# One PSUM bank request of the latents' attention, moved from the attention's banks to the projections' banks

## The chip, the cores and the metric

The kernel runs on one core of a Trainium2 chip. The metric is device time in microseconds (us) of one execution, from the first to the last instruction of the core with the little that lies around it. The time that is compared is the median of several executions.

## The reference

One inference step of a hybrid backbone with two layers. 128 context (prompt) tokens and 256 latent tokens share all weights. Each layer is a mixing sublayer (attention, a bidirectional mLSTM and a pooling, side by side, then one output projection) and a PEER expert sublayer:

```python
for l in range(DEPTH):                       # 2 layers
    h = rmsnorm(x) * (1 + scale1) + shift1
    x += gate1 * W_out[attention(h) | mlstm(h) | pool(h)]
    h = rmsnorm(x) * (1 + scale2) + shift2
    x += gate2 * peer(h)                     # 8 heads, top 16 of 16384 experts
y = rmsnorm(x)
```

What the change touches is the attention of the latents. 8 query heads share 2 key heads of width 64, the latents are two tiles of 128 tokens, and each tile attends to its own tile, to its neighbour under a band mask and to 128 cached context keys:

```python
s_band = einsum('bnqkgd,bnskd->bnkgqs', qb, kb) * scale    # masked outside the window
s_ctx  = einsum('bnqkgd,bpkd->bnkgqp', qb, kc) * scale
p = softmax_with_sink(concatenate([s_band, s_ctx], -1), sink)
o = p[..., :nband] @ vb + p[..., nband:] @ vc
```

The prompt tokens read only prompt tokens.

## The kernel before

**Stages.** For each layer `mixing` (line 352) computes the mixing sublayer for both groups of tokens, and also the prompt's half of the PEER routing; then come the latents' queries, scores and routing, and a dense PEER pass over all 16384 experts for the latents. In the dense pass TensorE multiplies blocks of 128 experts with all latents, while the prompt's 128 tokens are served by gathers on the GpSimd queue (`experts`, line 839) that are cut into small pieces and put between the other work.

**The order of the work.** `mixing` is a dictionary of steps, and two strings, `ORDER0` and `ORDER1` (lines 40 and 41), name the order in which the steps are written for layer 0 and layer 1. The steps that matter here: `att1` and `att2` are the attention of the two latent tiles, `att0` that of the prompt; `mem0`, `mem1`, `mem2` the mLSTM of the three tiles; `pool0`, `pool1` the pooling of the prompt and of the latents; `mix0` and `mix1` the output projection of the prompt and of the latents; `norm` the second norm of the prompt; `ask` the prompt's PEER queries and their top 16 (four groups, each a projection, a transposition and a score product); `route` the prompt's expert choice; `&mod1`, `mod1` and the like the modulation vectors, which stream 16 blocks of `w_mod` each; `+20` and the like run so many pieces of the prompt's experts. The strings are

```python
ORDER0 = "np ns kv c q gate qk ox | &mod1 mod1 mem2 mem0 mem1 att0 pool0 &mod2 att1 att2 pool1 mod2 &next0 mix0 spill norm ask mix1 next0 route +20 +3 +6 +3 +3"
ORDER1 = "np ns q c gate kv att0 qk ox &mod1 mod1 | mem0 pool0 &mod2 mod2 mix0 norm ask mem1 att1 spill route +5 +15 att2 mem2 pool1 +15 +10 mix1 +4"
```

The written order is a priority, not the final order: a planner (the tile framework's list scheduler with a timeline of its own) puts the instructions of each engine in a fixed order, earlier written ones first among those that are ready, and adds the waits. On the chip each engine runs its list in that order.

**PSUM.** A bank is 128 x 512 fp32. In the mixing stage the eight banks are four tags (`BANKS`, line 36): `at` with three, `pm` with one (modulation), `p` with three, `m` with one. `bank(tag, name)` (line 91) asks for a bank of a tag, and the planner hands it out when the tile is first written and takes it back after the last read. `p` serves the projections (`project` with its default tag), and by the step table `mem0`, `pool0`, `mix0`, `norm` and `ask`; `m` serves `mem1`, `mem2` and `pool1`; `at` serves `ns`, the query and key transposes, `att0`, `att1`, `att2` and `mix1`.

**The attention** is `attention(i, tag)` (line 640). For a latent tile it makes four passes, one for each of 2 key heads and 2 pairs of query heads. A pass is called a step below. A step takes two banks for the scores S (one per head, lines 664 to 668, each 128 x 384 with the mask added by a matmul), finds the row maxima on VectorE (668), forms the shift (670 to 672), exponentiates on ScalarE with the sum on the side (676), scales by the reciprocal sum on VectorE (681), transposes the six 128 x 128 blocks of probabilities on TensorE into two more banks PT (685 to 689), copies them to SBUF on ScalarE (690), and multiplies them with the values into the output bank `po`, written oT in the profile (692). `po` is held for all four steps of a tile. P has two SBUF buffers for the latents and PT three (`LAYOUT`).

**Other rings.** Weights pass through four raw buffers (`raw`), then are split by ScalarE (`hi`, line 105) and VectorE (`lo`, line 106) into four buffers each. The blocks of `w_mod` use the same four raw buffers. `rsqrt` (line 183) takes small tiles of tags `rs_v`, `rs_t` (two each) and `rs_r` (three).

Of the kernel before, what the change touches and what calls it, by code (L numbers as in the profile page):

```python
# [68 lines left out]
def tile_hybrid_step(ctx: ExitStack, tc: tile.TileContext, I, O):  # L69
# [21 lines left out]
    def bank(tag, name):  # L91
        tag = ALSO.get(tag, tag)
        pool, n = OPEN[tag]
        return pool.tile([P, 512], F32, tag=tag, bufs=n, name=name)
# [84 lines left out]
    def tsl(i):  # L179
        return slice(i * P, (i + 1) * P)  # L180
# [171 lines left out]
    def mixing(l, p1, rooms, silu):  # L352
# [169 lines left out]
        def mix_out(s, k0, k1, c, src):  # L522
            if s and mixT[1] is None:
                early.append((s, k0, k1, c, src))
                return
            if mixT[0] is None:
                mixT[0] = prompt_T(f"mixp{l}")
            split_into(*[t[:, k0:k1, c] for t in mixT[s]], src)
# [111 lines left out]
        def attention(i, tag):  # L640
            n = f"{i}{l}"
            room = rooms[min(i, 1)]
            ka = kaT[0] if i == 0 else kaT[1]
            vs = [kv[0][:, P:2 * P]] if i == 0 else [kv[1][:, P:2 * P], kv[2][:, P:2 * P], cv]
            nkp = len(vs)
            nk = nkp * P
            po = bank(tag, f"oT{n}")
            nh = 2 if i else 4
            for g in range(2):
                gs = slice(g * 64, g * 64 + 64)  # L650
                for j0 in range(0, 4, nh):
                    m = f"{n}{g}{j0}"
                    small = lambda tag: p1.tile([P, 4], F32, tag=f"{tag}{min(i, 1)}", bufs=2, name=f"{tag}{m}")[:, :nh]
                    mx, nm, es, sums = small("amx"), small("anm"), small("aes"), small("asum")
                    heads = []
                    if i == 0:
                        b = bank(tag, f"S{m}")
                        for j in range(4):
                            pe.matmul(b[:, tsl(j)], qaT[gs, j, tsl(i)], ka[gs, :], start=True, stop=True)
                            heads.append(b[:, tsl(j)])  # L660
                        ve.reduce_max(mx, b.rearrange("p (j k) -> p j k", j=4), axis=AX.X)
                    else:
                        for j in range(nh):
                            b = bank(tag, f"S{m}{j}")
                            pe.matmul(b[:, :nk], qaT[gs, j0 + j, tsl(i)], ka[gs, :], start=True, stop=False)
                            pe.matmul(b[:, tsl(2 - i)], identb, mskb[:, i - 1, :], start=False, stop=True)
                            heads.append(b[:, :nk])
                            ve.reduce_max(mx[:, j:j + 1], b[:, :nk], axis=AX.X)
                    sk = sinkb[:, g * 4 + j0:g * 4 + j0 + nh]
                    ve.scalar_tensor_tensor(nm, mx, 0.125, sk, op0=ALU.mult, op1=ALU.max)  # L670
                    ve.tensor_scalar_mul(nm, nm, -1.0)
                    ve.tensor_add(es, sk, nm)
                    ac.activation(es, es, AF.Exp)
                    Pt = room.tile([P, nh, nk], F32, "P", f"P{m}")
                    for j in range(nh):
                        ac.activation(Pt[:, j, :], heads[j], AF.Exp, bias=nm[:, j:j + 1], scale=0.125,
                                      accum_out=sums[:, j:j + 1])
                    ve.tensor_add(sums, sums, es)
                    ve.reciprocal(sums, sums)
                    for j in range(nh):  # L680
                        ve.tensor_scalar_mul(Pt[:, j, :], Pt[:, j, :], sums[:, j:j + 1])
                    PT = room.tile([P, nkp, nh * P], F32, "PT", f"PT{m}")
                    per = 512 // (nh * P)
                    for k0 in range(0, nkp, per):
                        b = bank(tag, f"PT{m}{k0}")
                        kps = range(k0, min(nkp, k0 + per))
                        for kp in kps:
                            for j in range(nh):
                                pe.transpose(b[:, tsl((kp - k0) * nh + j)], Pt[:, j, tsl(kp)], ident)
                        ac.copy(PT[:, k0:k0 + len(kps), :], b[:, 0:len(kps) * nh * P].rearrange("p (k x) -> p k x", k=len(kps)))  # L690
                    for kp in range(nkp):
                        pe.matmul(po[gs, j0 * P:(j0 + nh) * P], vs[kp][:, gs], PT[:, kp, :], start=(kp == 0),
                                  stop=(kp == nkp - 1), skip_group_check=True)
            mix_out(min(i, 1), 0, 4, tsl(max(i - 1, 0)), po.rearrange("p (j t) -> p j t", j=4))
# [35 lines left out]
        def mix(tiles, tag):  # L730
            room = rooms[min(tiles[0], 1)]
            g = gate_row(room, l, 0, min(tiles[0], 1))
            for h in range(2):
# [14 lines left out]
               for g, c in enumerate(cols) for w, t in who.items()},  # L748
            "|": collect,
            **{f"att{i}": (lambda i=i: attention(i, "at" if i else ATT0)) for i in range(3)},  # L750
            **{f"mem{i}": (lambda i=i: mlstm(i, "m" if i else "p")) for i in range(3)},
            "pool0": lambda: pooling(0, "p"),
# [591 lines left out]
```

## Time and profile before

| | us |
|---|---|
| median of 3 executions | 2735.05 |
| lowest, highest | 2731.38, 2752.36 |
| profiled execution, its own time | 2746.87 |
| its span, first to last instruction | 2745.1 |
| TensorE (PE) busy | 2500.7 (91%) |
| VectorE (DVE) busy | 1722.4 (63%) |
| ScalarE (ACT) busy | 1045.5 (38%) |
| GpSimd (POOL) busy | 927.6 (34%) |
| mean granted TensorE clock | 0.944 |

The profiled execution lies 11.8 us above the median and inside the span of the three times. Layer 0's mixing stage takes roughly the first 347 us, layer 1's roughly 1400 to 1717 us; the changed line runs at 176 to 282 us and 1500 to 1621 us. A busy TensorE is not one at its peak: matmuls overlap and their ends are modelled. "Granted clock" is the share of full TensorE speed.

### The profile page before, as it was taken

Reading aid. Unit: us, or ns where it says so; the run is one execution under the profiler, and the core shown is the slowest. Engines: PE = TensorE matmul, PEld = TensorE weight load, DVE = VectorE, ACT = ScalarE, POOL = GpSimd, SP = SyncE. Lnnn points to the kernel's source line nnn. Section 1 sums busy time; section 2 is a strip of 40 time slices with the busy share of each in tenths; the row PEclk is TensorE's granted clock in tenths of the full one; section 3 lists DMA queues with packets and bytes.
Section 4 is the critical chain, followed back from the end, with each engine's and each line's share of the span. In section 5 each row is a group of like instructions: output and inputs, shape, how many; then the busy total and the mean of one; then the engine's idle time right before and its main releaser. Section 6 shows DMA issues by size and latency. Waiting matters only on the chain.

```text
span 2745.1 us, 37514 instructions
## 1 busy us (share of the span) xinstructions
PE 2500.7 (91%) x13834; PEld 1915.5 (70%) x13834; DVE 1722.4 (63%) x3768; ACT 1045.5 (38%) x1545; POOL 927.6 (34%) x794
## 2 busy tenths in 40 slices
PE   7998779896999999999989885979969999999998
PEld 3744568785988777765666464868859877777665
DVE  4555979866877444443565468798778844444446
ACT  3434411544434433332444352114444433343333
POOL 0000034101445666754400002231224556656541
PEclk9998989897999999999999878999979999999999
DMA  7485589678899889897835644886999988888985
GB/s 258 139 269 194 167 289 337 210 268 321 305 352 347 303 314 330 290 330 259 292 122 166 218 162 152 315 291 232 334 347 353 329 296 311 299 315 289 330 294 192
DMA packets 217547, 749.33 MB, mean 273 GB/s; under 512 B 28308, under 2 KB 30868, under 8 KB 215316
## 3 DMA queue, kind: packets, MB, share of 16 engines
q1 hardware_dynamic: 137236, 444.91, 46.8%
q0 software_dynamic: 77824, 268.48, 27.9%
q10 hardware_dynamic: 2304, 33.56, 3.1%
q8 instruction: 108, 1.77, 0.3%
q14 instruction: 75, 0.61, 0.1%
HBM read 706.99 MB, written 39.85 MB: 272 GB/s over the span
## 4 chain that ended last, share of the span: by engine, by line
PE 62%; DMA 13%; DVE 12%; issue 7%; POOL 3%; ACT 2%; SPq 0%; POOLq 0%; DVEq 0%; ACTq 0%
PE po L134 22%; PE A L134 13%; PE pv L896 6%; DMA gu<-in_peer_u,ei 4%; PE A L1087 4%; PE pj_i L134 4%; DMA v_r<-in_peer_v 3%; DVE gu L883 3%; DMA gv<-in_v_half,eiT 2%; DMA wm<-in_w_mod 2%; PE pm L305 2%; POOL gu L863 2%; PE pj_t L134 2%; POOL gv L869 2%; PE pj_o L134 1%
## 5 line engine op out<-in xcount | busy, mean ns | idle before, releaser
L869 POOL DMA_INDIRECT gv<-in_v_half,eiT x512 | 590.1, 1153 | 437.7 <-PE pv L896 288.4
L134 PE MATMUL po<-v_h,W 128*128 128x512 f32 x2048 | 668.8, 398 | 30.5 <-ACT W L105 16.0
L863 POOL DMA_INDIRECT gu<-in_peer_u,ei x256 | 324.5, 1267 | 1095.0 <-DVE gu L883 474.6
L134 PEld LDWEIGHTS po<-v_h,W 128*128 128x128 f32 x2048 | 388.8, 191 | 160.7 <-ACT W L105 44.1
L106 DVE TENSOR_TENSOR v_l<-v_r,v_h 128x1024 fp32r<-128x1024 f32 x256 | 313.0, 1224 | 273.7 <-ACT v_h L105 273.5
L134 PE MATMUL A<-hs,u_h 128*128 128x256 f32 x2624 | 482.7, 284 | 1.3 <-ACT u_h L105 0.9
L134 PEld LDWEIGHTS A<-hs,u_h 128*128 128x128 f32 x2624 | 406.8, 189 | 58.9 <-issue 34.4
L105 ACT CAST v_h<-v_r 128x1024 fp32r<-128x1024 f32 x256 | 268.4, 1049 | 385.7 <-PE po L134 155.4
L134 PE MATMUL po<-v_l,W 128*128 128x512 f32 x1024 | 406.0, 397 | 0.1
L134 PE MATMUL A<-hs,u_l 128*128 128x256 f32 x1312 | 370.7, 283 | 2.4 <-DVE u_l L106 2.4
L106 DVE TENSOR_TENSOR u_l<-u_r,u_h 128x1024 fp32r<-128x1024 f32 x164 | 199.1, 1224 | 275.3 <-ACT u_h L105 275.2
L883 DVE SCALAR_TENSOR_TENSOR gu<-gu,h2n 128x1024 f32<-128x1024 f32 x256 | 307.4, 1218 | 63.7 <-DMA gu<-in_peer_u,ei 63.1
L1087 PE MATMUL A<-hw,u_r 128*128 128x256 f32 x1472 | 339.1, 386 | 0.0
L1087 PEld LDWEIGHTS A<-hw,u_r 128*128 128x128 f32 x1472 | 276.5, 193 | 36.0
L105 ACT CAST u_h<-u_r 128x1024 fp32r<-128x1024 f32 x164 | 171.4, 1050 | 307.8 <-PE A L134 258.5
L134 PEld LDWEIGHTS A<-hs,u_l 128*128 128x128 f32 x1312 | 248.3, 189 | 10.9 <-issue 6.7
L134 PEld LDWEIGHTS po<-v_l,W 128*128 128x128 f32 x1024 | 195.6, 191 | 49.6 <-issue 11.7
L896 PE MATMUL pv<-gv,wz 128*32 128x512 f32 x1024 | 194.2, 605 | 5.9 <-DVE wz L893 3.1
L106 DVE TENSOR_TENSOR W<-gl,W 128x512 fp32r<-128x512 f32 x128 | 87.9, 688 | 52.0 <-ACT W L105 51.9
L105 ACT CAST W<-gl 128x512 fp32r<-128x512 f32 x128 | 79.0, 618 | 105.7 <-PE po L134 72.0
L1089 ACT ACTIVATE gl<-A 128x512 f32<-128x512 f32 x128 | 75.5, 595 | 110.9 <-DVE W L106 62.9
L1046 PE MATMUL G<-o,o 128*128 128x128 f16 x1024 | 89.9, 238 | 30.0 <-DVE o L1038 27.6
(424 smaller groups left out, 2982.0 us busy)
## 6 DMA issues: line engine op xcount, KB each, us to landing
u_r<-in_u_T SPq DMA_DIRECT2D x256, 512.0 KB, 5.9
v_r<-in_peer_v SPq DMA_DIRECT2D x256, 512.0 KB, 5.1
wm<-in_w_mod SPq DMA_DIRECT2D x96, 512.0 KB, 5.7
gates<-stage ACTq DMA_DIRECT2D x14, 2048.0 KB, 10.9
G<-gates SPq DMA_DIRECT2D x16, 1792.0 KB, 12.4
w_o_r<-in_w_out SPq DMA_DIRECT2D x32, 512.0 KB, 4.6
w_q_r<-in_w_q SPq DMA_DIRECT2D x32, 512.0 KB, 5.5
w_i_r<-in_w_in SPq DMA_DIRECT2D x24, 512.0 KB, 4.5
```

What stands on the lines that cost most here:

```text
L105: ac.copy(hi, src)
L106: ve.tensor_sub(lo, src, hi.bitcast(F32))
L134: pe.matmul(out, a[x], b[y], start=first and n == 0, stop=last and n == 2, skip_group_check=True)
L305: pe.matmul(pm[32 * j:32 * j + 32, :], silu[:, kc, :], w[:, jj * 512:(jj + 1) * 512], start=(kc == 0), stop=(kc == KC - 1), skip_group_che ...
L863: gp.indirect_dma_start(out=t, out_offset=None, in_=I["peer_u"], in_offset=bass.IndirectOffsetOnAxis(ap=ei[:, k:k + 1], axis=0))
L869: gp.indirect_dma_start(out=t[:, j * 512:(j + 1) * 512], out_offset=None, in_=I["v_half"], in_offset=bass.IndirectOffsetOnAxis(ap=eiT[:, h ...
L883: behind(ve.scalar_tensor_tensor(u, u, 1.0, self.h2n, op0=ALU.mult, op1=ALU.mult, accum_out=dots[:, j:j + 1]))
L896: m = pe.matmul(self.acc[h][32 * q:32 * q + 32, :], wz[:, r % 8, q, :], v[q // 2][:, q % 2 * 512:q % 2 * 512 + 512], start=(r == 0), stop= ...
L1046: m = pe.matmul(pg[:, tsl(t)], o2[:, z, :, t0 + t], o1[:, t0 + t, :], start=(z == 0), stop=(z == 1), skip_group_check=True)
L1087: pe.matmul(out, u[:, tsl(k)], whole[:, k, :], start=k == 0, stop=k == KC - 1, skip_group_check=True)
L1089: ac.activation(gl, pa.rearrange("p (j t) -> p j t", j=2), AF.Gelu)
```

## The change

The bank for the transposed probabilities of the latents' attention (`i` is 1 or 2) is asked of the tag `p` and no longer of the attention's own tag `at`. The prompt's attention (`i` is 0) keeps its tag.

```diff
                     PT = room.tile([P, nkp, nh * P], F32, "PT", f"PT{m}")
                     per = 512 // (nh * P)
                     for k0 in range(0, nkp, per):
-                        b = bank(tag, f"PT{m}{k0}")
+                        b = bank("p" if i else tag, f"PT{m}{k0}")
                         kps = range(k0, min(nkp, k0 + per))
```

That is 2 banks in each of 4 steps of 2 tiles in 2 layers, 32 requests. No instruction is added, removed or resized.

## Rows read from the trace of the kernel before

**Rows 1.** The page, part 4: the chain that ended last, shares by engine.

```profile
PE 62%; DMA 13%; DVE 12%; issue 7%; POOL 3%; ACT 2%; SPq 0%; POOLq 0%; DVEq 0%; ACTq 0%
```

**Rows 2.** Busy time by stretch; columns from:to, length, each engine's busy, clock, DMA.

```profile
261.50:346.80 85.30, 61.38 (x310) 47.38 (x309) 75.09 (x288) 40.93 (x63) 1.12 (x1) 0.90 0.48 158
...
1484.00:1612.00 128.00, 111.65 (x490) 54.99 (x490) 62.45 (x178) 47.99 (x127) 2.30 (x3) 0.83 0.60 198
...
1586.00:1612.00 26.00, 24.41 (x68) 13.10 (x68) 9.69 (x45) 9.93 (x31) 0.00 (x0) 0.50 0.22 78
...
1664.20:1717.40 53.20, 20.64 (x93) 14.95 (x93) 46.31 (x189) 12.32 (x18) 14.60 (x13) 0.73 0.40 130
```

**Rows 3.** Timelines of PE and ACT, one attention step of layer 1; start, length.

```profile
1559.48 0.91 PE L665 MATMUL S<-kaT1s,qaT 64*128 64x384 f32 x2
...
1565.24 0.20 ACT L676 ACTIVATION_READ_ACCUMULATOR P<-S,anm 128x1 f32 x1
...
1567.94 0.81 PE L689 MATMUL PT<-ident,P 128*128 128x128 f32 x6
...
1572.59 0.91 PE L665 MATMUL S<-kaT1s,qaT 64*128 64x384 f32 x2
```

**Rows 4.** Timelines of PE and DVE, layer 1: the mLSTM of tile 1, then of tile 2.

```profile
1539.30 1.55 PE L590 MATMUL in<-nat,W 128*128 128x65 f32 x12
...
1547.26 0.42 DVE L613 TENSOR_REDUCE mms<-hr 128x4 f32<-128x256 f32 x1
...
1586.44 0.13 DVE L186 TENSOR_SCALAR rv_h21p<-ms_h21p 128x1 f32<-128x1 f32 x1
1586.49 0.16 DVE L186 TENSOR_SCALAR rv_ml<-mms 128x4 f32<-128x4 f32 x1
...
1595.92 0.64 PE L620 MATMUL mT<-ident,hm 128*128 128x128 f32 x2
...
1597.53 1.22 PE L547 MATMUL KQ<-qkT 64*128 64x128 f32 x4
```

**Rows 5.** Timeline of PE, layer 0: pool0's last, mix0's last, ask's first and last, two of mix1.

```profile
183.76 0.44 PE L725 MATMUL pq<-pd,pw 128*128 128x128 f32 x2
...
235.80 0.63 PE L134 MATMUL pj_o<-w_o_h,mixp 128*128 128x512 f32 x1
...
261.55 0.48 PE L134 MATMUL pj_q00p<-w_q00p_h,h2T 128*128 128x512 f32 x1
...
302.12 0.39 PE L134 MATMUL pj_o<-w_o_l,mixT 128*128 128x512 f32 x1
302.35 0.63 PE L134 MATMUL pj_o<-w_o_h,mixT 128*128 128x512 f32 x2
...
311.92 1.05 PE L808 MATMUL pss<-kT03p,qT03p 128*128 128x128 f32 x8
```

**Rows 6.** Timeline of PE, layer 1: ask, attention's last, mix1's last, the latents' next norm.

```profile
1612.15 0.77 PE L134 MATMUL pj_q01p<-w_q01p_h,h2T 128*128 128x512 f32 x1
...
1623.76 0.60 PE L692 MATMUL oT<-PT,cv 128*64 128x256 f32 x2
...
1661.74 1.05 PE L808 MATMUL pss<-kT13p,qT13p 128*128 128x128 f32 x8
...
1705.99 0.39 PE L134 MATMUL pj_o<-w_o_h,mixT 128*128 128x512 f32 x1
1717.37 1.56 PE L221 MATMUL pt_h<-ident,xn_h 128*128 128x128 f32 x6 [10.98 <-DVE xn_h L206]
```

**Rows 7.** Timeline of PE, layer 0: the shortest attention step.

```profile
259.03 0.91 PE L665 MATMUL S<-kaT0s,qaT 64*128 64x384 f32 x2
...
267.23 0.82 PE L689 MATMUL PT<-ident,P 128*128 128x128 f32 x6
...
270.51 0.91 PE L665 MATMUL S<-kaT0s,qaT 64*128 64x384 f32 x2
```

**Rows 8.** One tile: the VectorE half of a weight split; ns min/median/max.

```profile
L106 DVE TENSOR_TENSOR w_q10p_l<-w_q10p_r,w_q10p_h x4: 1219/1220/1226, 265.2 to 269.0; 128x1024 fp32r<-128x1024 f32 x4
```

## The prediction

> **What bounds the kernel now.** I read the page's chain first: TensorE is 62% of the chain that ended last, DMA and VectorE an eighth each [rows 1]. Most of that lies in the dense expert pass, which the change doesn't touch; what comes out of the two mixing stages later or earlier moves all that follows. So the second view is busy time by stretch [rows 2]. In layer 0 the end of the stage, 261.5 to 346.8 us, is VectorE's: 75.1 of 85.3 us busy, TensorE 61.4. In layer 1 TensorE is 111.7 of 128.0 us busy up to 1612, at a granted clock of 0.83; 1586 to 1612 runs wholly at the lower level (0.50, that is 1.2 GHz). From 1664 to 1717 VectorE leads (46.3 of 53.2) while TensorE waits.
>
> The third view is the timeline of one step of the attention [rows 3]. S starts at 1559.48, the exponentials have been read at 1565.44 (1565.24 + 0.20): from then on the two S banks are free. The next step's S starts only at 1572.59, after the transposes and their copies. For 7.15 us two free banks stood idle beside ready operands; they were kept for PT, the next request of that tag in the written order. The shortest whole step of the trace shows the same: S 259.03, PT 267.23, next S 270.51, so 11.48 us [rows 7].
>
> The rows that decide are another ring [rows 4]. Tag `m` has one bank. The mLSTM of tile 1 wrote its last sum at 1539.30 and didn't touch the bank again until mT at 1595.92; the KQ products of tile 2, whose operands were ready, came at 1597.53, not in the 55 us between. And tile 1's small `rsqrt` tile, ready at 1547.68, was written at 1586.49, 0.05 us after that of the prompt's norm, which is written earlier in the string. I conclude that a tag is handed out in the written order and that nobody overtakes.
>
> **The change part by part.** It removes nothing and adds nothing; it moves 32 bank requests from one queue to another. I cost the two sides, per layer, as shifts of that layer's end.
>
> *What the attention wins.* The S banks no longer wait for PT. A step's period is then bounded below by S to the exponentials' end, 1565.44 - 1559.48 = 5.96 us [rows 3], and above by the shortest whole step, 11.48 us [rows 7]. I take 8.5: the engines are shared, so the lower end won't be met, and the upper is what the change undoes. The first step of each tile keeps its full 11.5, since the output bank is first written behind PT and is asked for ahead of the second step's S.
>
> *What layer 0 pays.* The string has `mem0 ... pool0 ... att1 att2 ... mix0 norm ask`. PT now stands in `p` behind pool0 and ahead of mix0. Pool0's last product is at 183.76 [rows 5]; PT to the next S takes 270.51 - 267.23 = 3.3 us [rows 7], so the second S comes at 187.5. Then three periods (25.5), tile 2's first step (11.5) and two periods (17) lead to the last S at 241.5, and its PT, 267.23 - 259.03 = 8.2 later, at 249.7. Only then may mix0 have its bank; today it has finished at 236.4 [rows 5]. Its first half (24 matmuls) finds its weights split; the second half's four splits take 1.22 each [rows 8]; with some 6 us for each half it ends at about 263, 26.5 late. From mix0's end to ask's first matmul is 25.1 us now [rows 5]; I take 17, because two attention steps no longer stand in TensorE's list there (bounds 12 and 25). So ask starts at 280 instead of 261.55.
>
> Then something is given back. Ask takes 50.4 us now [rows 5], with attention and half of mix1 in between. Alone, four groups of about 9.6 us (24 matmuls at 0.23, the distance of two starts in [rows 5], and an estimated 4 for two round trips to ScalarE) make 38. VectorE bounds the rest: its 75.1 busy us [rows 2] lose about three steps of attention at 2.7 each, 67 remain, and at today's density (0.88) they last 76. From 280 that is 356, against 346.8: **9 us late**. With a period of 5.96 mix0 starts 12.7 us sooner (five periods), and the layer ends 4 early; with 11.48 it is 24 late.
>
> *What layer 1 pays.* Here the string has `mix0 norm ask mem1 att1 ... route +5 +15 att2`, so all of ask stands ahead of att1's first PT. Today the attention ends at 1624.4 while ask runs from 1612.15 to 1662.8 [rows 6]. After the change the attention does one step's scores and stops until the last `pss` of ask has its bank. Ask gains: 7 of 8 steps leave the 128 us up to 1612 and with them part of the stretch at the lower clock [rows 2]; I take 25 us (bounds 10 and 35; by today's stretch the 16.4 us without TensorE work and half of the 26 us at the lower clock would be 29). Ask then starts at 1587 and, at 40 us (38 and some of tile 2's mLSTM), gives PT its first bank at 1627. From there: 3.3 to the second S, 25.5, 11.5 and 17 to the last S, 8.2 to its PT and 4 to its last product: 1697, against 1624.4. Mix1 needs the attention's rows first; of its 96 matmuls some 78 remain (18 us), so it ends at 1716 against 1706.4 [rows 6]. The prompt's gathers, 20 pieces written ahead of att2, now wait on VectorE between att2's steps; I add 5 (0 to 15). **15 us late**; with period 5.96, ask 35 early and no gathers 13 early, with 11.48, ask 10 early and the full gathers 55 late.
>
> A rule of the Trainium skill speaks for the change: in "Perfetto Trace Analysis", Optimizing Tensor Performance, independent matmul groups should rotate through different PSUM banks, so that one's evacuation overlaps the next one's matmuls. The 7.15 us of [rows 3] agree with it as to the attention itself; by the rule alone the sum would be only what the attention wins, the first rival below.
>
> The sum is 9 + 15 = 24 us on the profiled execution's 2746.9, that is 2771. That execution lies 11.8 above the median of 2735.05, so the median comes to **2759**, 0.9% slower. The dense pass follows the stages without slack, so I carry the shifts through in full.
>
> **The rivals.**
> - *More banks simply help* (the rotating rule). If the request order does not bind across steps, PT fits between the projections' uses, the attention loses about 7 us in each of 6 steps per layer, and TensorE fills its stalls. The steps overlap other work today, so only stalls come back: half of the 26 us at the lower clock in layer 1, 13, and about as much in layer 0 at its attention stalls: 26 less, 2709. For it: S banks idle beside ready work. Against it: [rows 4], where a bank idle for 55 us was not lent. It decides if mix0 of layer 0 still ends near 236.
> - *The serial chain is worse than I sum.* Alone on TensorE the attention runs at the lower clock, and VectorE's list holds it behind route and gathers. The upper ends are 24 + 55 = 79 us: about 2799 with part of it (64). For it: 0.50 at 1586 to 1612 [rows 2], with attention in it. Against it: VectorE's own work gets no longer.
> - *It evens out.* Ask in layer 1 gets 35 us earlier and VectorE, the bound at both ends, has the same work: within 5 us, 2735. For it: VectorE's 46.3 of 53.2 [rows 2]. Against it: att2 would have to end before 1685.
>
> The Trainium skill, "TensorE: Matmul & The Clock Gate", Why this matters for your kernels, warns that idle gaps between matmul bursts send the clock back to its lower level. Our 1586 to 1612 stretch shows 0.50 with TensorE 94% busy by the rows; by the rule an attention left alone would stay there, as in the second rival.
>
> **How the numbers follow.** Forecast (5 to 45 us more) 0.45; worse 0.2; evens out 0.18; more banks help 0.17. A measurement of this kernel tells about 1%, 27 us, from no change. Slower by over 1%: the upper half of the forecast (0.22) and the worse case (0.2), 0.42. Faster by over 1%: under half of the first rival and a little of unlooked-for orders, 0.11. The rest 0.47. The forecast's own range is 2740 to 2780; over all cases 2712 to 2797.
>
> **What would show it.** Right: in layer 0 no mix0 matmul before the attention's last PT, and mix0 ending near 263; in layer 1 the attention's first PT right behind ask's last `pss`, near 1627, ask's first matmul near 1587, the attention's end near 1697, and S following S after 6 to 11 us within a tile. Wrong: mix0 ending near 236 or a latent PT near 1500 would say that the order does not bind; an attention in layer 1 that ends before 1680 or after 1715 would move the size.

## The result, and the profile after

The changed kernel takes 2769.12 us (median of 11 runs, 2759.52 to 2777.91), the kernel before 2741.77 in the same comparison (11 runs, 2731.38 to 2752.45). The ratio is 1.0096, 95% interval 1.0075 to 1.0118: about 27 us slower. The forecast was 24 us. The two profiled executions differ by 21.4 us of span (2766.5 against 2745.1). So the sum came out close. The places where it is paid did not.

The first view of after is TensorE's timeline in layer 0, from the prompt's pooling to the first queries; it answers to [rows 5, 7].

```profile
179.20 0.49 PE L725 MATMUL pq<-pd,pw 128*128 128x128 f32 x2
179.52 0.82 PE L689 MATMUL PT<-ident,P 128*128 128x128 f32 x6
...
182.43 0.91 PE L665 MATMUL S<-kaT0s,qaT 64*128 64x384 f32 x2
...
239.17 0.91 PE L665 MATMUL S<-kaT0s,qaT 64*128 64x384 f32 x2
...
244.97 0.41 PE L689 MATMUL PT<-ident,P 128*128 128x128 f32 x2 [0.94 <-DVE P L681]
245.14 0.48 PE L134 MATMUL pj_o<-w_o_h,mixp 128*128 128x512 f32 x1
...
260.73 0.40 PE L134 MATMUL pj_o<-w_o_h,mixp 128*128 128x512 f32 x1
...
280.05 0.80 PE L134 MATMUL pj_q00p<-w_q00p_h,h2T 128*128 128x512 f32 x1
```

This is the written order of `p`, to a fraction of a microsecond: PT's first bank 0.32 us after the start of `pool0`'s last product, `mix0`'s first matmul 0.17 us after the last PT bank is first written. Between them lie the 16 PT banks of the layer. `mix0` had started at 184.77 before (the row below); now it starts 60 us later and lasts 16 us instead of 52.

```profile
184.77 0.50 PE L134 MATMUL pj_o<-w_o_h,mixp 128*128 128x512 f32 x1
```

Layer 1, the same engine, from the last score product of `ask` to the attention's end; it answers to [rows 3, 6].

```profile
1629.16 1.16 PE L808 MATMUL pss<-kT13p,qT13p 128*128 128x128 f32 x8 [0.73 <-ACT qT13p L803]
1630.16 0.82 PE L689 MATMUL PT<-ident,P 128*128 128x128 f32 x6
...
1632.55 0.91 PE L665 MATMUL S<-kaT1s,qaT 64*128 64x384 f32 x2
...
1640.34 1.59 PE L665 MATMUL S<-kaT1s,qaT 64*128 64x384 f32 x2 [3.65 <-ACT P L676]
...
1675.66 1.65 PE L665 MATMUL S<-kaT1s,qaT 64*128 64x384 f32 x2
...
1687.09 1.64 PE L665 MATMUL S<-kaT1s,qaT 64*128 64x384 f32 x2 [6.71 <-ACT P L676]
...
1697.81 1.05 PE L665 MATMUL S<-kaT1s,qaT 64*128 64x384 f32 x2 [2.45 <-ACT P L676]
...
1715.40 0.59 PE L692 MATMUL oT<-PT,cv 128*64 128x256 f32 x2
1757.64 1.56 PE L221 MATMUL pt_h<-ident,xn_h 128*128 128x128 f32 x6 [13.04 <-DVE xn_h L206]
```

The attention of layer 1, which had ended at 1624.4, now begins its second step at 1632.55 and ends at 1716.0. The latents' next norm comes 40.3 us later than before (1717.37), and in between TensorE waits again and again, for ScalarE's exponentials in three of the rows above and for VectorE's scaling elsewhere (4.59 us ahead of the PT at 1648.53).

Where does the rest of the time go? I cut both spans at the same six events: the first S of the latents in layer 0, the latents' next norm (`pt_h`), the first gated product of the dense pass (line 1097), the first scores of the prompt in layer 1, then again `pt_h` and the first gated product. Busy time by these stages, the kernel before; columns are from:to, length, busy time of TensorE, its weight load, VectorE, ScalarE and GpSimd, granted clock, DMA share, GB/s:

```profile
160.01:347.61 187.60, 153.96 (x696) 90.09 (x695) 126.77 (x438) 82.15 (x165) 1.81 (x2) 0.88 0.58 193
347.61:681.57 333.96, 285.24 (x1686) 250.99 (x1686) 257.22 (x729) 115.37 (x172) 82.30 (x75) 0.89 0.82 289
681.57:1451.77 770.20, 742.89 (x4173) 572.96 (x4173) 442.76 (x597) 303.72 (x370) 380.16 (x316) 0.98 0.84 293
1451.77:1717.37 265.60, 214.46 (x993) 136.84 (x992) 165.53 (x547) 102.39 (x227) 16.91 (x16) 0.86 0.53 174
1717.37:2040.74 323.37, 282.70 (x1686) 248.50 (x1686) 263.75 (x740) 114.86 (x172) 83.34 (x78) 0.92 0.84 301
2040.74:2745.10 704.36, 683.73 (x3922) 526.99 (x3922) 389.08 (x484) 270.70 (x316) 360.35 (x297) 0.98 0.86 302
```

The same stages, after:

```profile
162.21:359.20 196.99, 154.92 (x697) 92.53 (x696) 127.09 (x438) 83.25 (x165) 1.82 (x2) 0.86 0.56 183
359.20:680.65 321.45, 282.53 (x1686) 248.74 (x1686) 257.26 (x730) 116.41 (x172) 84.04 (x75) 0.91 0.82 293
680.65:1448.57 767.92, 741.88 (x4172) 572.53 (x4172) 442.41 (x597) 303.71 (x370) 376.68 (x316) 0.98 0.84 297
1448.57:1757.64 309.07, 236.84 (x992) 148.28 (x992) 186.75 (x585) 104.80 (x227) 38.44 (x35) 0.79 0.56 184
1757.64:2063.30 305.66, 281.72 (x1686) 248.28 (x1686) 241.08 (x702) 115.43 (x172) 65.92 (x59) 0.94 0.80 283
2063.30:2766.50 703.20, 681.47 (x3922) 526.67 (x3922) 388.94 (x484) 271.10 (x316) 356.56 (x297) 0.99 0.86 303
```

Read the lengths downwards. Layer 0's mixing stage is 9.4 us longer, and the stage behind it 12.5 shorter: nothing of it is left at the first gated product (680.65 against 681.57). Layer 1's is 43.5 longer and the next 17.7 shorter. Those are the two places where a shift is given back. First, VectorE at that product of layer 0, before and after:

```profile
681.57 1.29 DVE L1097 TENSOR_TENSOR gl<-gl,G 128x512 f32<-128x512 f32 x2 [13.62 <-DMA G<-gates]
```

```profile
680.65 1.29 DVE L1097 TENSOR_TENSOR gl<-gl,G 128x512 f32<-128x512 f32 x2 [4.24 <-DMA G<-gates]
```

Before, VectorE had waited 13.62 us there for the gates to come back from memory. After, it comes later and waits 4.24. I took this to mean that the wait takes up the delay, and the expectations of the first runs rest on it. The traces say otherwise, for the load reads what the late stage itself has spilled to memory. Here is the stage cut where the last spill ahead of that load is issued, before:

```profile
347.61:655.31 307.70, 277.53 (x1624) 244.48 (x1624) 244.91 (x709) 107.86 (x161) 77.27 (x71) 0.93 0.81 284
655.31:681.57 26.26, 7.71 (x62) 6.52 (x62) 12.32 (x21) 7.51 (x11) 5.03 (x5) 0.50 0.92 347
```

And after:

```profile
359.20:659.40 300.20, 274.17 (x1622) 242.04 (x1622) 240.52 (x703) 108.92 (x161) 76.37 (x69) 0.94 0.80 287
659.40:680.65 21.25, 8.37 (x64) 6.70 (x64) 16.75 (x28) 7.49 (x11) 7.67 (x7) 0.53 1.00 384
```

Of the 12.5 us, 7.5 are made up ahead of the spill and 5.0 behind it, and 4.4 us of VectorE's work (244.91 - 240.52) stand behind the spill instead of ahead of it. In all five profiles with layer 0's requests in `p`, norm to product takes 319 to 321 us; in the other nine it takes 330 to 336. And a stage that is late for another reason gets little back: in the control with two banks in `p` (below) the norm came 19.7 us later than before and the product still 16.8, behind a wait of 11.43. So layer 0's shift is given back by a stage whose work the planner put in another order; why that order is shorter was not shown.

Second, the prompt's gather products (line 883, two records each: the product and its accumulated sum), the stage up to the norm and the stage behind it, before:

```profile
1451.77:1717.37 265.60, 9.76 (x16) 14.60 (x13) 0.86 0.53 174
1717.37:2040.74 323.37, 95.31 (x156) 83.34 (x78) 0.92 0.84 301
```

And after, the first of them cut out of the attention's late part:

```profile
1630.00:1716.00 86.00, 20.93 (x34) 21.44 (x20) 0.64 0.46 141
...
1448.57:1757.64 309.07, 33.11 (x54) 36.13 (x32) 0.79 0.56 184
1757.64:2063.30 305.66, 72.09 (x118) 65.92 (x59) 0.94 0.80 283
```

27 gather products (54 records) stand ahead of the norm instead of 8, and 23.35 us of VectorE's time (33.11 - 9.76) have moved from behind the norm to ahead of it. That delays the norm and is given back afterwards: 95.31 - 72.09 = 23.2. Of layer 1's 43.5 us about half is such moved work, and some 22 us stay, as the first gated product of layer 1 shows (2063.30 - 2040.74 = 22.6, though the stage had begun 3.2 us sooner).

My theory when I planned the runs, called A below: the order of the requests in `p` makes one queue of the attention and the projections; layer 0 pays for it out of a wait that is there anyway, layer 1 pays in full. The rivals: both layers' shifts add (B, the forecast's own bookkeeping); it is not the order but PT among the projections as such (C); it is the gathers (P below, against Q).

### The profile page after: what moved, and what is told of

Its sections match the earlier page's. It is cut to its first block, busy times and chain, and to the rows that moved or that the text cites. A ratio compares the mean times of both kernels' runs of the same rounds, so it can differ in the third digit from the quotient of the medians.

```text
span 2766.5 us, 37544 instructions
## 1 busy us (share of the span) xinstructions
PE 2518.1 (91%) x13834; PEld 1926.2 (70%) x13834; DVE 1720.9 (62%) x3768; ACT 1051.0 (38%) x1545; POOL 926.2 (33%) x794
## 4 chain that ended last, share of the span: by engine, by line
PE 61%; DMA 12%; issue 11%; DVE 10%; POOL 3%; ACT 2%; SPq 0%; POOLq 0%; DVEq 0%; ACTq 0%
PE po L134 23%; PE A L134 13%; PE pv L896 6%; PE pj_i L134 4%; DMA gu<-in_peer_u,ei 3%; DMA wm<-in_w_mod 3%; DMA v_r<-in_peer_v 3%; PE A L1087 3%; POOL gu L863 2%; DVE gu L883 2%; PE pj_q L255 2%; PE pm L305 2%; DMA gv<-in_v_half,eiT 2%; PE pj_t L134 2%; POOL gv L869 1%
## 5 line engine op out<-in xcount | busy, mean ns | idle before, releaser
L869 POOL DMA_INDIRECT gv<-in_v_half,eiT x512 | 582.2, 1137 | 442.8 <-PE pv L896 293.7
L863 POOL DMA_INDIRECT gu<-in_peer_u,ei x256 | 330.9, 1293 | 1113.6 <-DVE gu L883 507.7
L134 PEld LDWEIGHTS po<-v_l,W 128*128 128x128 f32 x1024 | 195.1, 191 | 48.8 <-issue 10.9
L255 PE MATMUL pj_q<-hw,w_q_r 128*128 128x256 f32 x512 | 116.6, 390 | 0.9 <-DVE hw L225 0.9
```

What stands on the lines that cost most here:

```text
L134: pe.matmul(out, a[x], b[y], start=first and n == 0, stop=last and n == 2, skip_group_check=True)
L255: pe.matmul(pj[:, 0:n], w[:, tsl(k)], rhs(k), start=k == 0, stop=k == KC - 1, skip_group_check=True)
L863: gp.indirect_dma_start(out=t, out_offset=None, in_=I["peer_u"], in_offset=bass.IndirectOffsetOnAxis(ap=ei[:, k:k + 1], axis=0))
L869: gp.indirect_dma_start(out=t[:, j * 512:(j + 1) * 512], out_offset=None, in_=I["v_half"], in_offset=bass.IndirectOffsetOnAxis(ap=eiT[:, h ...
```

## The experiments

**One layer alone** (the edit against the changed kernel).

```diff
-                        b = bank("p" if i else tag, f"PT{m}{k0}")
+                        b = bank("p" if i and l == 0 else tag, f"PT{m}{k0}")
```

> The changed bank request in layer 0 alone; layer 1 keeps the old tag. Theory A (the requests queue in the written order in both layers, but what layer 0 loses is taken back at the first gate load of the dense pass): mix0 of layer 0 ends near 261, the latents' next norm comes near 359 instead of 347.6, the first gated product near 681 as before, and the time is within 5 us of before (ratio 0.998 to 1.002). Rival B (both layers' shifts add, as the forecast had it): +9 to +12 us, ratio 1.003 to 1.0045.

2769.48 us against 2742.82 (ratio 1.0082, 1.0053 to 1.0111): neither. Layer 0 alone costs as much as the whole change, and both expectations fall.

With `l == 1` instead:

> The changed bank request in layer 1 alone. Theory A: the whole of the change's +26 us is here: +20 to +28, ratio 1.007 to 1.010, first latent PT of layer 1 directly behind ask's last pss. Rival B: +15 us, ratio 1.0055, the rest being layer 0's. Rival C (the loss is not in the order of the requests but any PT in the projections' banks costs it): cannot be told from A here; the run with the attention written earlier tells them apart.

2766.92 us (1.0069, 1.0037 to 1.0100), +24: what theory A wanted. But the two layers alone together make far more than both at once, so the parts don't simply add, and something else than the two queues is in the first run. Its stages show where to look:

```profile
174.52:370.50 195.98, 154.08 (x697) 92.09 (x696) 127.21 (x438) 83.35 (x165) 1.82 (x2) 0.86 0.57 185
370.50:689.35 318.85, 282.81 (x1686) 248.84 (x1686) 257.49 (x729) 115.93 (x172) 82.25 (x75) 0.92 0.83 296
...
1459.60:1735.02 275.42, 213.43 (x993) 138.04 (x992) 173.34 (x561) 102.91 (x227) 25.43 (x23) 0.84 0.56 185
```

And its gather products in the last of these (VectorE's and GpSimd's busy time):

```profile
1459.60:1735.02 275.42, 18.44 (x30) 23.13 (x20) 0.84 0.56 185
```

Layer 1's stage is 9.8 us longer than before (275.42 against 265.60), although nothing was edited there: 15 gather products stand ahead of the norm instead of 8. The tile 2 mLSTM also got another place in VectorE's list; its `mms` comes ahead of the routing's top 16 before (first row), and here behind them (second row):

```profile
1662.37 0.42 DVE L613 TENSOR_REDUCE mms<-hr 128x4 f32<-128x256 f32 x1
```

```profile
1679.23 0.41 DVE L613 TENSOR_REDUCE mms<-hr 128x4 f32<-128x256 f32 x1
```

The planner lays out the engines' lists for the whole program, so an edit in layer 0 can change the order of unedited work in layer 1. How much of the +27 this is, the profile can't tell: it is 14.4 us longer than that of before (2759.5 against 2745.1), and it is 14.5 us late already at the first latent S, ahead of every changed instruction.

**The attention of layer 1 written earlier**, with the new tag and, as a control, with the old one.

```diff
-... | mem0 pool0 &mod2 mod2 mix0 norm ask mem1 att1 spill route +5 +15 att2 mem2 pool1 +15 +10 mix1 +4"
+... | mem0 pool0 att1 att2 &mod2 mod2 mix0 norm ask mem1 spill route +5 +15 mem2 pool1 +15 +10 mix1 +4"
```

> The changed kernel with att1 and att2 of layer 1 written right behind pool0, ahead of mod2, mix0 and ask. Theory A (the written order of the requests in p decides): the first latent PT of layer 1 comes right behind the first scores near 1495, all eight steps are done before ask's first product, at 1575 to 1610, ask starts at 1585 to 1615, the latents' next norm comes at 1715 to 1735 instead of 1757.6, and the time is 2730 to 2750, some 20 to 35 below the change. Rival C (PT in the projections' banks itself costs the time): within 5 us of the change, 2764 to 2774.

> The same written order in layer 1 with the old bank tag, the control of the run before it. Theory A: the old tag lets the attention run as soon as its operands are there whatever stands in p, so the order alone changes little: 2730 to 2752, ratio 0.996 to 1.004. If the new order alone gains or loses more than 10 us, the difference between this run and the one before it, and not that run by itself, is the tag's.

With the new tag 2767.99 us (1.0086, 1.0052 to 1.0119), with the old one 2748.24 (1.0018, 0.9997 to 1.0039). The places came out as theory A had them (steps done near 1576, `ask` at 1607.4, the norm at 1727.5), all but one: the first PT doesn't come near 1495. The time did not come down; it is rival C's. TensorE's timeline of the new tag in this order says why:

```profile
1481.39 0.91 PE L665 MATMUL S<-kaT1s,qaT 64*128 64x384 f32 x2
...
1517.55 0.44 PE L725 MATMUL pq<-pd,pw 128*128 128x128 f32 x2
1517.83 0.82 PE L689 MATMUL PT<-ident,P 128*128 128x128 f32 x6
...
1575.65 0.41 PE L689 MATMUL PT<-ident,P 128*128 128x128 f32 x2
1575.82 0.47 PE L134 MATMUL pj_o<-w_o_h,mixp 128*128 128x512 f32 x1
```

The attention stands 36 us behind `pool0`, then `mix0` stands behind the attention, each going on within 0.3 us of the row above it. `mix0` starts 129.4 us into the stage (1575.82 - 1446.41) and in the control 106.9 (1561.42 - 1454.50); the stage takes 281.1 us against 267.0. Another order only changes who waits. The same early order with the change in layer 1 alone was to take layer 0 out of it:

> The changed request in layer 1 alone, with att1 and att2 of layer 1 written right behind pool0. Theory A (order of requests decides in layer 1, and the time that the early run with both layers still lost is layer 0's): 2738 to 2755, that is within 7 us of its control with the old tag (2748) and 15 to 28 below layer 1 alone in the old order (2767). Rival C (PT in the projections' banks costs it wherever it is written): 2762 to 2772.

2766.27 us against 2738.55 (1.0104, 1.0075 to 1.0134), as the rival had it: here `mix0` waits for the last PT until 1588.03, and the stage takes 287.9 us. So "the order decides" falls as I had put it. What stands is narrower, and I call it theory S: the tag makes the attention and the projections one queue, they no longer overlap, and no written order that was tried gives that back.

**The gathers last.** To take the moved gather products out of the comparison, all pieces of layer 1 are written behind `mix1`, with the change and without it:

```diff
-... spill route +5 +15 att2 mem2 pool1 +15 +10 mix1 +4"
+... spill route att2 mem2 pool1 mix1 +5 +15 +15 +10 +4"
```

> The changed kernel with all pieces of the prompt's gathers of layer 1 written behind mix1. In VectorE's list the gather products ahead of the latents' next norm fall from 27 to 3 (8 in the kernel before). Theory P (the late attention of layer 1 is charged mostly by the gather products that VectorE's list puts between its steps): that norm's transposition comes at 1725 to 1740 instead of 1757.6, the attention's last product at 1690 to 1705 instead of 1715.4, but the gathers are paid after it, so the first gated product of layer 1 comes only 0 to 10 us sooner than 2063 and the time is 2755 to 2768. Theory Q (the queueing behind ask alone sets it): the norm at 1750 or later, the time unchanged within 4 us.

> The same late gathers in the kernel before, the control: products ahead of the norm fall from 8 to 3. Theory P: the norm some 5 us earlier, the gathers 10 us later, the time 2738 to 2752 (ratio 0.998 to 1.004). Theory Q: no difference either.

The changed kernel: 2765.75 us (1.0096, 1.0068 to 1.0123), the attention's last product at 1689.6 and the norm at 1723.61. The kernel before: 2735.20 (0.9995, 0.9973 to 1.0017), the norm at 1707.03. So theory P is nearly right about the norm's place (1725 was its bound) and right that it is worth almost nothing at the end: 34 us sooner at the norm, some 3 us in the median, at the same ratio of 1.0096. The price of the change is unaltered, 30 us between these two. In the control the gathers were not paid later, as P had it; its first gated product of layer 1 came 11 us earlier than before.

At this order of the gathers, each layer alone (the two by two table):

> The change in layer 0 alone, gathers of layer 1 written last. With the two runs that wrote the gathers last this makes a two by two table at one order of the gathers (neither layer 2735, both 2766). Theory S (the tag makes one queue of the attention and the projections; in layer 0 the price of about 13 us is paid out of the wait for the first gate load, 13.6 us long before, and only what a run is late beyond it goes through; the +27 of layer 0 alone came from layer 1's list, where the planner put 15 gather products instead of 8 ahead of the norm): layer 0's stage 196 to 203 us from the first latent S to the norm, layer 1's stage 253 to 260 us as in the control, the time 2735 to 2748. Rival D (layer 0's price reaches the end whatever layer 1 does): 2755 to 2766.

> The change in layer 1 alone, gathers of layer 1 written last. Theory S: layer 1's stage 267 to 275 us against the control's 255, the time 2748 to 2762, which is most of the 30 us between the control and the change at this order. Rival D: 2740 to 2750, layer 0 carrying the other half.

| gathers last | us | ratio to before, interval |
|---|---|---|
| neither layer | 2735.20 | 0.9995, 0.9973 to 1.0017 |
| layer 0 alone | 2751.62 | 1.0031, 1.0013 to 1.0050 |
| layer 1 alone | 2764.48 | 1.0095, 1.0067 to 1.0122 |
| both | 2765.75 | 1.0096, 1.0068 to 1.0123 |

The rows come from two comparisons, each with its own executions of the kernel before, so the ratios are what to compare.

Layer 0 alone falls from 1.0082 to 1.0031 by an edit of layer 1's order only: much of its +27 hung on layer 1's order. Some 10 us remain, more than theory S had (it wanted 2748 at most). Layer 1 alone carries the whole change, a little more than S had. By the ratios layer 0 costs some 10 us by itself and nothing more beside layer 1, but the intervals are too wide to tell whether the two add at this order. Stages of layer 0 alone, then of layer 1 alone, then layer 1's stage of the control (neither) and of both:

```profile
163.31:364.29 200.98, 158.29 (x697) 93.59 (x696) 127.24 (x438) 83.04 (x165) 1.81 (x2) 0.83 0.55 179
364.29:684.72 320.43, 281.83 (x1686) 247.89 (x1686) 257.05 (x729) 115.61 (x172) 83.53 (x75) 0.92 0.82 294
...
1452.97:1713.48 260.51, 208.68 (x993) 135.05 (x992) 158.86 (x537) 102.75 (x227) 10.62 (x11) 0.86 0.53 171
```

```profile
1448.52:1735.78 287.26, 230.30 (x992) 144.86 (x991) 158.85 (x537) 104.49 (x227) 10.61 (x11) 0.82 0.47 156
1735.78:2059.69 323.91, 282.81 (x1686) 248.45 (x1686) 268.79 (x750) 115.43 (x172) 91.28 (x83) 0.92 0.85 304
```

```profile
1451.94:1707.03 255.09, 207.06 (x993) 133.78 (x992) 159.95 (x537) 102.22 (x227) 10.87 (x11) 0.89 0.54 175
```

```profile
1454.06:1723.61 269.55, 217.33 (x993) 138.64 (x992) 158.51 (x537) 104.11 (x227) 10.59 (x11) 0.86 0.50 166
```

Layer 1's 32 us (287.26 - 255.09) have the same VectorE work in them (158.85 against the control's 159.95) and are not given back: the next stage takes 323.91 against 322.70. That is the queue's price without any moved work, and more than the 267 to 275 us that S had for the stage. It is no constant: with both layers changed, at the same order of the gathers, the stage is 14.5 us longer than the control's and the next one 5.4 (328.09 against 322.70). There PT has its first bank 169.0 us into the stage (1623.02 - 1454.06) instead of 181.6 (1630.16 - 1448.52); why is not shown.

**A bank of its own.** PT gets an eighth bank of the mixing stage, and the projections keep two; as a control the projections have two and the eighth bank lies idle.

```diff
-BANKS = (dict(p=3, m=1), dict(A=2, pv=2), dict(at=3, pm=1))
+BANKS = (dict(p=2, m=1, x=1), dict(A=2, pv=2), dict(at=3, pm=1))
...
-                        b = bank(tag, f"PT{m}{k0}")
+                        b = bank("x" if i else tag, f"PT{m}{k0}")
```

> PT gets one bank of its own in both layers, in no queue with other work; the projections keep two of their three. Theory A (the loss is the queue in p, not the removal from at): attention steps follow within a tile after 6 to 10 us in layer 0 and layer 1, mix0 of layer 0 ends before 245, the last latent product of layer 1 before 1610, VectorE's list has 10 gather products ahead of the norm, and the time is 2725 to 2750. Rival (the projections need their third bank): slower than 2755, with TensorE waiting for copies of projections or of PT.

> The kernel before with two banks for the projections instead of three and the eighth bank unused, the control of PT's own bank (2748). Theory S: the lost bank costs more than PT's own bank gives back, so this one is 2752 to 2775, and the attention's own gain from PT's separate bank is the difference, 5 to 25 us. Rival (a bank of its own gives the attention nothing, since ScalarE and VectorE set the step): 2745 to 2750, no difference.

Own bank: 2748.26 us (1.0041, 1.0020 to 1.0062). Two banks and none for PT: 2767.01 against 2741.90 (1.0094, 1.0069 to 1.0118). The intervals don't meet: PT's separate bank is worth 0.5%, some 14 us, and the projections' third bank 0.9%, some 25. The first is paid where the attention runs: layer 0's stage takes 179.1 us against the control's 189.1, layer 1's 259.2 against 267.8. The second lies ahead of it: the first latent S comes at 178.1 to 179.0 us in the three profiles with two banks in `p`, at 160.0 before and at 162.2 in the changed kernel. So the change's 27 us are not the price of that third bank, although PT leaves the projections fewer banks at a time. In the own-bank run `mix0` of layer 0 runs among the attention's products (201.46 to 250.05), where the change had it behind them. `mix0`'s end missed the bound of 245 that I had set; this run's first 178 us were already 18 late. Nor did the steps follow each other after 6 to 10 us within a tile; they took 5.7 to 27.2.

> PT's own bank with the gathers of layer 1 written last, the candidate for a version that beats both. The profile with the own bank had layer 0's stage at 179.1 us (187.6 before) and layer 1's at 259.2 (265.6), and its first 178 us were late by some 15. Theory S: 2733 to 2748, at best level with the kernel before. Rival (the two gains add): below 2730.

2743.34 us (1.0000, 0.9979 to 1.0020): level with the kernel before. No version here beats it beyond the interval.

## Why the prediction was right in its sum, and where it was not

**The ring is handed out in the written order.** Right, in both layers and in both written orders of layer 1: each release is followed within 0.3 us (layer 0's 179.52 and 245.14, the early order's 1517.83 and 1575.82) or 1.0 us (1630.16).

**Layer 0's steps.** Right one after the other: second S 182.4 (said 187.5), last S 239.2 (241.5), `mix0`'s end 261.1 (263), `ask` at 280.05 (280), the stage 9.4 longer (9). The six steps from the second S to the last took 56.7 us, 54 in the forecast (five of 8.5 and one of 11.5).

**Carrying layer 0's shift to the end.** This step failed: "The dense pass follows the stages without slack, so I carry the shifts through in full." The 9.4 us were gone at the first gated product, since the stage behind became 12.5 us shorter, with its work in another order; the forecast had kept that stage as it was. The two by two table leaves some 10 us of layer 0 alone. In that run's profile 2.7 us of lateness are left at the first gated product and 5.4 more arise in layer 1's stage against the control; what makes these was not shown.

**Layer 1's steps up to the first PT.** Right: `ask` at 1586.0 (1587), PT at 1630.2 (1627).

**Layer 1's term of +15.** Mis-sized in two of its parts. The period: the six steps from the S at 1632.55 to that at 1697.81 took 65.3 us, 10.9 each, where the forecast had 54. The gathers: "I add 5 (0 to 15)" was 20.93 us of products between 1630 and 1716, laid by VectorE's list between the steps, so that the two parts overlap. The attention ended at 1716 instead of 1697 and the norm was 40 us late instead of 15. Of that 22.6 reached the first gated product: the moved gathers came back, which the forecast had not counted either. So +24 was reached as 0 + 22 and not as 9 + 15: that the sum is close is luck, one term 9 too large and the other 7 too small. And the two prices don't add: with the gathers in their old place either layer alone cost nearly as much as both.

**The rivals.** *More banks simply help* is out as a result, but its mechanism is in the two control runs: a bank outside anybody's queue gave 14 us. *It evens out*, meant for layer 1, has its like in the changed kernel's layer 0, though only in the stage behind the norm. *The serial chain is worse* was the right direction for layer 1, too high in all.

**Rotating through banks, and the clock.** In the runs a separate bank for PT gained 14 us and PT in the projections' banks lost 27. The rule of the Trainium skill, "Perfetto Trace Analysis", Optimizing Tensor Performance, to rotate through different banks, agrees with the first of these and not with the second: the bank was different, but its queue belonged to others.

In the changed kernel the granted clock is 0.64 from 1630 to 1716, where the attention has TensorE nearly to itself and leaves it idle for 25.9 of the 86 us, and 0.79 in that whole stage against 0.86 before. The S at 1632.55 takes 0.91 us; the one at 1640.34, behind 3.65 us of waiting, takes 1.59. The warning of the Trainium skill, "TensorE: Matmul & The Clock Gate", Why this matters for your kernels, that idle gaps send the clock back to its lower level, agrees with this.

## What to carry to other kernels

A PSUM tag is a queue as much as a set of banks: before moving a request to a tag with idle banks, write down what stands ahead of it and behind it in that tag, for what is behind it now waits for its chain. A shift of a stage is not yet a shift of the end: follow it to a fixed event further on (here the first gated product). A long wait there doesn't show that the shift is taken up, when what is waited for hangs on the late stage itself (a lateness of 19.7 us came through the wait for the gates with 16.8 left). And where a planner lays out the lists, compare variants at a fixed place of movable work (here the gathers), or the planner's new choices elsewhere will be counted as the edit's own.

## What the runs showed that I had not expected

The time of one and the same kernel follows its mean granted clock. Of the 28 executions of the kernel before that ran beside the own-bank run, the five with 0.950 or more took 2727.4 to 2733.1 us, the five with 0.943 or less 2738.3 to 2748.9. The mean over those 28 was 0.9466; over the 11 of the changed kernel 0.9395. The means of the two fives lie 12.6 us and 0.0078 apart, so by these runs I estimate that 11 or 12 of the change's 27 us go with the clock. That the clock is their cause was not tried by itself.

A stretch at a lower clock can also fall where nothing was changed. In the profile of layer 0 alone, with the gathers in their old place, the granted clock was 0.65 from 120 to 174 us, ahead of every changed instruction, and the first latent S came at 174.5 instead of 160 to 166 in the other kernels with three banks in `p`. At the first gated product 8.7 us of it were left against the changed kernel (689.35 and 680.65). Whether layer 0's remaining 10 us have to do with the clock, no run here shows.
